# The mixer of a hybrid S5 and mLSTM layer: conv halo in the row, decay masked before the exp, S5 tables at half width copied by DMA, tokens of a block by position

## The chip, the cores and the metric

The kernel runs on one core of one Trainium2 chip. The core has five engines with queues of their own: PE (matrix products into PSUM), DVE (VectorE), ACT (ScalarE), POOL (GpSimd) and SP, which here issues all DMAs. Each engine takes its instructions in order, and semaphores make one engine wait for another. The metric is the time of one execution on the device in microseconds; lower is better. Times shown are medians of several runs; a profile is one more execution with the profiler on.

## What is computed

One layer (DEPTH = 1) over a sequence of 2048 tokens of width 1024, all in float32: a norm, one combined projection whose columns feed two mixers, an output projection, and a feed-forward block of width 4096.

```python
h = rmsnorm(x, norm_mix_g);  p = h @ w_in
u, q_raw, k_raw, v, o_raw, i_raw, f_raw = split(p)
# S5: 32 groups of 16 channels, 64 complex states a group
x_t = ab * x_{t-1} + (bb @ u_t)              # bb = s * b, complex, per group
y = Re(c @ x_t) + d * u
z = gelu(y); z = z * sigmoid(z @ w_glu + b_glu); y_ssm = rmsnorm(z)
# mLSTM: 4 heads of 128
q, k = split(silu(causal_conv_width_4([q_raw, k_raw]) + conv_b))
dmat = where(mask, bcum_t - bcum_s + i_s, -inf)
s = (q k^T) * exp(dmat - m_t)
num = s v + exp(inter - m_t) * (q C);  h = num / max(|den|, exp(-m_t))
C = decay * C + sum_s wk_s k_s v_s
y_ml = rmsnorm(sigmoid(o_raw) * h)
x = x + concat(y_ssm, y_ml) @ w_out
x = x + relu(rmsnorm(x) @ w_ff1)^2 @ w_ff2
out = rmsnorm(x)
```

## The kernel before

The sequence is cut into 4 blocks of 512 tokens (TB); with 4 heads that makes 16 mixer blocks, numbered b = 4 * head + token block. Products that must be near float32 are made of three float16 matmuls on a high and a low half of each operand (mm3, L152; its three lines are L156, L157, L158). Transposes and the small products of the mixers are float32 matmuls.

The program is written as Python that lists instructions; a planner then orders each engine's queue by its own model of time and sets the semaphores. So instructions of neighbouring steps lie mixed in each queue, and a buffer with `bufs=1` makes the next writer wait for the last reader.

In time order:

- **Start.** norm_x normalises and transposes x. u_proj makes S5's input u into uz, proj_vo and proj_qk start on the first blocks. s5_tables (L289) builds, on DVE, the powers of the state matrix (pwr, pwi) and cosine and sine tables: Lc, Ls, Hc, Hs hold the angles of 16 low and 16 high steps for all 32 groups on all 128 partitions; the lower 64 partitions stand for the real and the upper 64 for the imaginary part, and L403 turns the sign of Ls and Hs in the upper half.
- **Mixer blocks, 0 to 15** (the loop near the end of the mixer part). Block b has proj_qk for block b + 1 (L222), mix_store for block b - 1 (L879), mix_scores (L800), proj_vo (L245), mix_state (L827) and mix_out (L850). In blocks 0 to 10, 16 S5 units of two groups each are mixed in: s5_state(u) (L655), s5_const(u + 1) (L566) and s5_out(u) (L692), one or two units a block. In blocks 11 to 15 and after them come 16 GLU steps (glu_a, glu_b, glu_c), and the loads of the output weights (load_wo).
- **Output projection** (out_proj), with the last GLU steps beside it, and then the **feed-forward** block, over half of the time.

The steps that the change touches:

- *Conv in proj_qk.* The product pq lies in PSUM, channels by tokens. ACT makes y = w3 * pq + bias (L231). DVE adds the three other taps by shifted reads of pq (L233, 511, 510 and 509 columns), and after each the tap of the one to three columns that come from the block before (L235, from the tile hl, which L238 keeps). Then ACT's tanh (L241) and DVE's product (L242).
- *mix_scores.* bcm holds minus the running maximum, spread over partitions by DMA. For each of four chunks DVE makes min(bcm + g, 0) (L808), then ACT takes exp of all four at once (L812), and POOL sets what lies above the diagonal to 0 (L813, affine_select).
- *s5_const.* Per unit: one DMA of B and C for two groups (L580), seven small DVE instructions of 32 columns that scale them (six through the helper at L577, and L594), products with powers, two small PE steps, and the unit's cosT and sinT: 512 columns, three instructions on POOL (L574) and three on DVE (L577), each from L and H tables by broadcast. cosT and sinT have one buffer.
- *s5_state.* The product pw is turned by cosT and sinT (L676, L677, L678), scanned (L681), turned back (L685, L686). ACT exchanges the two halves of the partitions by copies (L674, L675, L683, L684); the sign is in the tables.
- *s5_out.* ACT squares py, DVE makes 0.044715 * y2 + 1 (L704) and multiplies by py (L705), ACT takes the tanh (L706), and so on.
- *glu_c.* The transposed GLU result is split into float16 halves in ms: L782 on ACT and L783 on DVE, both with the token index as outer and step 8 in the output.
- *mix_store.* The transposed head output is split likewise into mo (L887, L888), straight, and stored by DMA (L889).

## Time and profile before

| | |
|---|---|
| runs, median (3 runs) | 2251.63 us (2249.8 to 2255.08) |
| profiled execution, own time | 2252.2 us |
| its span, first to last instruction | 2250.5 us |
| mean granted clock of PE | 0.966 |
| matrix instructions, DVE, ACT, POOL instructions | 11021, 3087, 1799, 1039 |
| busy share of the span: PE, DVE, ACT, POOL | 92%, 81%, 47%, 50% |

How to read the views: a group's row gives line, engine, operation, out<-in with partitions x columns and type, its count, then busy microseconds in all and mean nanoseconds of one, then the idle time just ahead of it and who ended that. A row of the stretches gives start and end, the length, the busy time and number of instructions of each engine, the granted clock, the DMA engines' share and their GB/s. A row of the timeline gives start, duration, engine, line and the instruction. A busy PE is not a PE at its peak, since matmuls overlap in the record; how far apart they start tells what they cost. SPq is SP's sequencer, which issues DMAs.

### The profile page before, as it was taken

How to read it: one execution, taken by the hardware profiler on the slowest of the kernel's cores; microseconds unless marked ns; L12 is line 12 of the kernel's file. 1: busy time of each engine (PE TensorE's matmuls, PEld its weight loads, DVE VectorE, ACT ScalarE, POOL GpSimd, SP SyncE). 2: the span in 40 equal slices, each digit the busy share in tenths (PEclk: the TensorE clock that was granted, in tenths of full speed). 3: DMA queues.
4: the chain of work that ended last, by engine and by line, in shares of the span. 5: the costliest groups of instructions: out<-in, count | busy, mean ns of one | idle time of the engine just before them, and what ended most of it. 6: DMA issues, size and time to landing. Idle time of an engine off the chain costs nothing.

```text
span 2250.5 us, 29559 instructions
## 1 busy us (share of the span) xinstructions
PE 2063.3 (92%) x11021; PEld 1155.6 (51%) x11021; DVE 1813.9 (81%) x3087; ACT 1059.5 (47%) x1799; POOL 1132.4 (50%) x1039
## 2 busy tenths in 40 slices
...
GB/s 171 60 34 31 36 13 17 55 17 16 80 15 31 175 57 47 75 131 173 47 71 57 57 57 57 57 56 187 113 150 99 119 86 54 75 38 75 38 20 93
DMA packets 48624, 159.75 MB, mean 71 GB/s; under 512 B 6944, under 2 KB 16352, under 8 KB 35936
## 3 DMA queue, kind: packets, MB, share of 16 engines
...
## 4 chain that ended last, share of the span: by engine, by line
PE 50%; DVE 27%; DMA 6%; POOL 3%; issue 3%; ACT 3%; SPq 0%; POOLq 0%; DVEq 0%; ACTq 0%
PE gx L1281 4%; PE gx L1283 4%; PE gx L1282 4%; PE fx L1281 4%; PE fx L1282 4%; PE fx L1283 4%; PE gv L1281 2%; PE gv L1282 2%; PE gv L1283 2%; PE fv L1283 2%; PE fv L1282 2%; PE fv L1281 2%; DVE y L233 2%; DMA r<-in_w_dram 2%; PE po L156 2%
## 5 line engine op out<-in xcount | busy, mean ns | idle before, releaser
L1159 ACT ACTIVATE w2o<-r,fs_b 128x512 f16<-128x512 f32 (+1 forms) x128 | 105.4, 824 | 153.6 <-PE gx L1283 75.1
L1310 ACT ACTIVATE e<-e 128x512 f32<-128x512 f32 x96 | 60.3, 629 | 210.8 <-DVE e L1350 95.2
L1282 PEld LDWEIGHTS <-w2o 128*128 128x128 f16 x896 | 87.7, 98 | 132.2 <-issue 31.3
L1160 DVE SCALAR_TENSOR_TENSOR w2o<-r,fs_b,w2o 128x512 f16<-128x512 f32 (+1 forms) x128 | 130.3, 1019 | 27.3 <-ACT w2o L1159 27.1
L1281 PEld LDWEIGHTS <-w2o 128*128 128x128 f16 x896 | 87.9, 98 | 108.3 <-issue 2.9
L1283 PEld LDWEIGHTS <-w2o 128*128 128x128 f16 x896 | 87.7, 98 | 106.4 <-DVE w2o L1160 1.1
L156 PE MATMUL pv<-w_vo,xn 128*128 128x256 f16 x512 | 141.1, 276 | 0.3 <-ACT xn L433 0.3
L158 PE MATMUL pv<-w_vo,xn 128*128 128x256 f16 x512 | 140.9, 275 | 0.4 <-DVE xn L434 0.3
L157 PE MATMUL pv<-w_vo,xn 128*128 128x256 f16 x512 | 141.0, 275 | 0.0
L1216 POOL TENSOR_TENSOR r<-r,s 128x256 f32<-128x256 f32 x64 | 62.6, 978 | 130.5 <-DVE w2o L1160 129.2
L1380 DVE SCALAR_TENSOR_TENSOR x2b<-gx,dd,x2b 128x512 f32<-128x512 f32 x128 | 94.7, 744 | 41.2 <-PE gx L1283 41.0
L1281 PE MATMUL fx<-hop,wB 128*128 128x512 f16 x256 | 98.0, 383 | 9.8 <-ACT e L1339 7.7
L1380 DVE SCALAR_TENSOR_TENSOR x<-gx,dd,x 128x512 f32<-128x512 f32 x128 | 94.6, 743 | 14.7 <-PE gx L1283 14.6
L156 PE MATMUL pq<-xn,w_qk 128*128 128x512 f16 x256 | 99.1, 388 | 0.0
L158 PE MATMUL pq<-xn,w_qk 128*128 128x512 f16 x256 | 98.9, 386 | 0.0
L157 PE MATMUL pq<-xn,w_qk 128*128 128x512 f16 x256 | 98.6, 385 | 0.0
L1282 PE MATMUL fx<-hop,wB 128*128 128x512 f16 x256 | 98.0, 383 | 0.0
L1283 PE MATMUL fx<-hop,wB 128*128 128x512 f16 x256 | 97.8, 382 | 0.0
L157 PEld LDWEIGHTS <-xn 128*128 128x128 f16 x768 | 87.9, 115 | 11.2 <-issue 2.1
L1173 POOL TENSOR_TENSOR s<-r 128x512 f32<-128x512 f32 x32 | 55.3, 1729 | 76.0 <-issue 72.8
L156 PEld LDWEIGHTS <-xn 128*128 128x128 f16 x768 | 87.8, 114 | 10.7 <-ACT xn L433 1.2
L158 PEld LDWEIGHTS <-xn 128*128 128x128 f16 x768 | 87.7, 114 | 8.3 <-DVE xn L434 0.9
...
## 6 DMA issues: line engine op xcount, KB each, us to landing
...
hopd<-ho SPq DMA_DIRECT2D x28, 256.0 KB, 2.4
...
bcm<-negM_d SPq DMA_DIRECT2D x16, 256.0 KB, 3.2
ml_d<-mo SPq DMA_DIRECT2D x16, 256.0 KB, 2.3
```

Of the source, the lines that this page charges most:

```text
L156: T.matmul(out, wh, xh, start=(i == 0), stop=False)
L157: T.matmul(out, wh, xl, start=False, stop=False)
L158: T.matmul(out, wl, xh, start=False, stop=(i == n - 1))
L1159: S.activation(out=hi, in_=src, func=AF.Copy, scale=sg)
L1160: V.scalar_tensor_tensor(out=lo, in0=src, scalar=sg, in1=hi, op0=ALU.mult, op1=ALU.subtract)
L1173: G.tensor_tensor(out=s12[:, 0], in0=raw[:, 2], in1=raw[:, 3], op=ALU.add)
L1216: G.tensor_tensor(out=r[:, 1], in0=r[:, 1], in1=s12[:, 1], op=ALU.subtract)
L1281: T.matmul(out, wh, xh, start=(first and i == 0), stop=False, skip_group_check=True)
L1282: T.matmul(out, wh, xl, start=False, stop=False, skip_group_check=True)
L1283: T.matmul(out, wl, xh, start=False, stop=(last and i == n - 1), skip_group_check=True)
L1310: S.activation(out=x, in_=x if src is None else src, func=AF.Relu, scale=scale)
L1380: V.scalar_tensor_tensor(out=acc[:, j, c, :], in0=bk[b], scalar=dd, in1=acc[:, j, c, :], op0=ALU.mult, op1=ALU.add)
```

## The change

- *Conv.* ACT also copies pq into an SBUF row xc of 515 columns; the first three are the halo, copied by POOL from hl or set to zero at a head's first block, and POOL keeps the next halo from xc. The three taps then read xc over all 512 columns; the small taps and the copy on DVE go.
- *Decay.* POOL's affine_select comes first, from bcm with -1e30 above the diagonal; ACT then makes the exp per chunk with g as bias. The DVE step with its min goes.
- *S5 B/C.* Every fourth unit, s5_bc loads and scales B and C for eight groups at once.
- *Tables.* L and H tables are kept for one of a unit's two groups in each half of the partitions, so they are half as wide; a unit's cos and sin are made once as rh (256 columns each), and four DMAs copy them into rt, which has two buffers, once for each half of the partitions and group. The sign is no longer in the tables: two of ACT's copies take scale -1.
- *s5_out.* One DVE instruction makes (y2 + 1/0.044715) * py, and tanh's scale takes up the factor.
- *Token order.* Within a block of 512 tokens the order is by position within eight, then by eight: glu_c writes runs of 64, mix_store reads the transposed tile in steps of 8, and the host lays x and the output out to fit.

```diff
@@ -35,6 +35,7 @@
 S5_BLOCKS = 11
+RT_BUFS = 2
@@ -228,15 +229,20 @@
         wc = cw[:, 4 * w:4 * w + 4]
...
+        xc = mpa.tile([P, TB + 3], F32, name=f"xc{nm}{w}", tag="xc", bufs=2)
+        S.activation(out=xc[:, 3:], in_=pq, func=AF.Copy)
         S.activation(out=y, in_=pq, func=AF.Identity, scale=wc[:, 3:4], bias=cb[:, w:w + 1])
-        for j in range(1, 4):
-            V.scalar_tensor_tensor(out=y[:, j:], in0=pq[:, :TB - j], scalar=wc[:, 3 - j:4 - j], in1=y[:, j:], op0=ALU.mult, op1=ALU.add)
-            if t > 0:
-                V.scalar_tensor_tensor(out=y[:, 0:j], in0=halo[w][:, 3 - j:3], scalar=wc[:, 3 - j:4 - j], in1=y[:, 0:j], op0=ALU.mult, op1=ALU.add)
+        if t > 0:
+            G.tensor_copy(xc[:, 0:3], halo[w])
+        else:
+            G.memset(xc[:, 0:3], 0.0)
...
             hl = smal.tile([P, 3], F32, name=f"hl{nm}{w}", tag=f"hl{w}", bufs=2)
-            V.tensor_copy(hl, pq[:, TB - 3:TB])
+            G.tensor_copy(hl, xc[:, TB:TB + 3])
             halo[w] = hl
+        for j in range(1, 4):
+            V.scalar_tensor_tensor(out=y, in0=xc[:, 3 - j:3 - j + TB], scalar=wc[:, 3 - j:4 - j], in1=y, op0=ALU.mult, op1=ALU.add)
@@ -271,10 +277,10 @@
     pwi = cp.tile([P, 9, NG], F32, name="pwi")
-    Lc = cp.tile([P, 16, NG], F32, name="Lc")
-    Ls = cp.tile([P, 16, NG], F32, name="Ls")
-    Hc = cp.tile([P, 16, NG], F32, name="Hc")
-    Hs = cp.tile([P, 16, NG], F32, name="Hs")
+    Lc = cp.tile([P, 16, 16], F32, name="Lc")
+    Ls = cp.tile([P, 16, 16], F32, name="Ls")
+    Hc = cp.tile([P, 16, 16], F32, name="Hc")
+    Hs = cp.tile([P, 16, 16], F32, name="Hs")
@@ -384,23 +390,26 @@
-            t3 = dp.tile([P, 8, NG], F32, name="t3")
...
+            cs2, sn2 = (dp.tile([P, 8, 16], F32, name=f"d_{n}") for n in ("cs2", "sn2"))
+            for o_, i_ in ((cs2, cs), (sn2, sn)):
+                for g in range(2):
+                    hp_ = slice(64 * g, 64 * g + 64)
+                    V.tensor_copy(o_[hp_], i_[hp_, 1:9].rearrange("p l (u g) -> p l g u", g=2)[:, :, g])
+            t3 = dp.tile([P, 8, 16], F32, name="t3")
...
                     n = 1 << l
-                    ec = cs[:, 1 + 4 * b + l, :].unsqueeze(1).to_broadcast([P, n, NG])
-                    es = sn[:, 1 + 4 * b + l, :].unsqueeze(1).to_broadcast([P, n, NG])
+                    ec = cs2[:, 4 * b + l, :].unsqueeze(1).to_broadcast([P, n, 16])
+                    es = sn2[:, 4 * b + l, :].unsqueeze(1).to_broadcast([P, n, 16])
...
                     add(s_[:, n:2 * n], s_[:, n:2 * n], t3[:, :n])
-            for s_ in (Ls, Hs):
-                fl = s_.rearrange("p l g -> p (l g)")
-                V.tensor_scalar(out=fl, in0=fl, scalar1=sgn, scalar2=None, op0=ALU.mult)
@@ -562,6 +571,24 @@
     s5 = s5_ctx.enter_context(pool("s5"))
+    bcs = {}
...
+    def s5_bc(v):
...
+        bcA = bcs[v] = s5.tile([P, 4, 8, 16], F32, name=f"bcA{v}", tag="bcA", bufs=2)
+        nc.sync.dma_start(out=bcA, in_=s5bc[:, :, 8 * v:8 * v + 8, :])
+        bt = [s5.tile([P, 8, 16], F32, name=f"bt{v}{i}", tag="bt", bufs=2) for i in range(2)]
...
+        def mul(o, a, b):
+            V.tensor_tensor(out=o, in0=a, in1=b[:, 8 * v:8 * v + 8].unsqueeze(2).to_broadcast([P, 8, 16]), op=ALU.mult)
...
+        mul(bt[0], bcA[:, 1], ssi)
+        mul(bt[1], bcA[:, 0], sim)
+        mul(bcA[:, 0], bcA[:, 0], sre)
+        mul(bcA[:, 1], bcA[:, 1], ssr)
+        V.tensor_tensor(out=bcA[:, 0], in0=bcA[:, 0], in1=bt[0], op=ALU.add)
+        V.tensor_tensor(out=bcA[:, 1], in0=bcA[:, 1], in1=bt[1], op=ALU.subtract)
+        V.tensor_scalar(out=bcA[:, 2], in0=bcA[:, 2], scalar1=sgn, scalar2=None, op0=ALU.mult)
@@ -576,22 +603,9 @@
-        bc = st("bc", (4, 2, 16), 2)
-        nc.sync.dma_start(out=bc, in_=s5bc[u])
...
-        eb, fb, tb_ = st("eb", (2, 16)), st("fb", (2, 16)), st("tb", (2, 16))
...
-        def b16(a):
-            return a[:, gs].unsqueeze(2).to_broadcast([P, 2, 16])
...
-        vtt(eb, bc[:, 0], b16(sre), ALU.mult)
-        vtt(tb_, bc[:, 1], b16(ssi), ALU.mult)
-        vtt(eb, eb, tb_, ALU.add)
-        vtt(fb, bc[:, 1], b16(ssr), ALU.mult)
-        vtt(tb_, bc[:, 0], b16(sim), ALU.mult)
-        vtt(fb, fb, tb_, ALU.subtract)
-        cg = st("cg", (2, 16))
-        V.tensor_scalar(out=cg, in0=bc[:, 2], scalar1=sgn, scalar2=None, op0=ALU.mult)
+        if u % 4 == 0:
+            s5_bc(u // 4)
+        eb, fb, cg, cx = (bcs[u // 4][:, i, 2 * (u % 4):2 * (u % 4) + 2, :] for i in range(4))
@@ -633,22 +647,26 @@
-        cosT, sinT = st("cosT", (2, 16, 16), 1), st("sinT", (2, 16, 16), 1)
-        tc_, td_ = st("t1", (2, 16, 16)), st("t2", (2, 16, 16))
+        rh = st("rh", (2, 16, 16))
+        tc_, td_ = (st(t, (2, 16, 16))[:, 0] for t in ("t1", "t2"))
...
         def hk(a):
-            return a[:, :, gs].rearrange("p k g -> p g k").unsqueeze(3).to_broadcast([P, 2, 16, 16])
+            return a[:, :, u].unsqueeze(2).to_broadcast([P, 16, 16])
...
         def ll(a):
-            return a[:, :, gs].rearrange("p k g -> p g k").unsqueeze(2).to_broadcast([P, 2, 16, 16])
...
-        gtt(cosT, hk(Hc), ll(Lc), ALU.mult)
+            return a[:, :, u].unsqueeze(1).to_broadcast([P, 16, 16])
...
+        gtt(rh[:, 0], hk(Hc), ll(Lc), ALU.mult)
         gtt(tc_, hk(Hs), ll(Ls), ALU.mult)
-        gtt(cosT, cosT, tc_, ALU.subtract)
-        vtt(sinT, hk(Hs), ll(Lc), ALU.mult)
+        gtt(rh[:, 0], rh[:, 0], tc_, ALU.subtract)
+        vtt(rh[:, 1], hk(Hs), ll(Lc), ALU.mult)
         vtt(td_, hk(Hc), ll(Ls), ALU.mult)
-        vtt(sinT, sinT, td_, ALU.add)
-        s5u[u] = xt, m0, inT, cosT.rearrange("p g k l -> p (g k l)"), sinT.rearrange("p g k l -> p (g k l)")
+        vtt(rh[:, 1], rh[:, 1], td_, ALU.add)
+        rt = st("rt", (2, 2, 256), RT_BUFS)
+        for g in range(2):
+            for h in range(2):
+                nc.sync.dma_start(out=rt[64 * h:64 * h + 64, g], in_=rh[64 * g:64 * g + 64].rearrange("p s k l -> p s (k l)"))
+        s5u[u] = xt, m0, inT, rt[:, :, 0, :], rt[:, :, 1, :]
@@ -669,24 +687,23 @@
             T.matmul(pw_[:, g, :], inT[:, g, :], us[:, g].rearrange("p h c -> p (h c)"), start=True, stop=True)
-        wf = pw_.rearrange("p g c -> p (g c)")
-        t1, t2 = st("t1", (512,)), st("t2", (512,))
-        S.copy(t2[0:64], wf[64:128])
-        S.copy(t2[64:128], wf[0:64])
-        V.tensor_tensor(out=t1, in0=wf, in1=cosF, op=ALU.mult)
...
+        t1, t2 = st("t1", (2, 256)), st("t2", (2, 256))
+        S.copy(t2[0:64], pw_[64:128])
+        S.activation(out=t2[64:128], in_=pw_[0:64], func=AF.Copy, scale=-1.0)
+        V.tensor_tensor(out=t1, in0=pw_, in1=cosF, op=ALU.mult)
...
         for g in range(2):
-            gc = slice(g * 256, (g + 1) * 256)
-            V.tensor_tensor_scan(out=t1[:, gc], data0=R8[:, g0 + g:g0 + g + 1].to_broadcast([P, 256]), data1=t1[:, gc], initial=0.0, op0=ALU.mult, op1=ALU.add)
-        t2 = st("t2", (512,))
+            V.tensor_tensor_scan(out=t1[:, g], data0=R8[:, g0 + g:g0 + g + 1].to_broadcast([P, 256]), data1=t1[:, g], initial=0.0, op0=ALU.mult, op1=ALU.add)
+        t2 = st("t2", (2, 256))
         S.copy(t2[0:64], t1[64:128])
-        S.copy(t2[64:128], t1[0:64])
+        S.activation(out=t2[64:128], in_=t1[0:64], func=AF.Copy, scale=-1.0)
...
         G.memset(sv[:, :, 0:1], 0.0)
-        G.tensor_tensor(out=sv[:, :, 1:257], in0=t1.rearrange("p (g c) -> p g c", g=2), in1=t2.rearrange("p (g c) -> p g c", g=2), op=ALU.subtract)
+        G.tensor_tensor(out=sv[:, :, 1:257], in0=t1, in1=t2, op=ALU.subtract)
@@ -701,9 +718,8 @@
         S.activation(out=y2, in_=py, func=AF.Square)
-        V.tensor_scalar(out=y2, in0=y2, scalar1=0.044715, scalar2=1.0, op0=ALU.mult, op1=ALU.add)
-        V.tensor_tensor(out=y2, in0=y2, in1=py, op=ALU.mult)
-        S.activation(out=y2, in_=y2, func=AF.Tanh, scale=GC)
+        V.scalar_tensor_tensor(out=y2, in0=y2, scalar=1.0 / 0.044715, in1=py, op0=ALU.add, op1=ALU.mult)
+        S.activation(out=y2, in_=y2, func=AF.Tanh, scale=GC * 0.044715)
@@ -778,9 +794,10 @@
             T.transpose(pT[:, m, :], zc[:, m * P:(m + 1) * P], ident)
-        mv = ms[h].rearrange("p s m (c i) -> p s i m c", i=8)
-        S.activation(out=mv[:, 0, i], in_=pT, func=AF.Copy)
-        V.tensor_tensor(out=mv[:, 1, i], in0=pT, in1=mv[:, 0, i], op=ALU.subtract)
+        mv = ms[h].rearrange("p s m (b i c) -> p s i m b c", b=2, i=8)
+        pv_ = pT.rearrange("p m (b c) -> p m b c", b=2)
+        S.activation(out=mv[:, 0, i], in_=pv_, func=AF.Copy)
+        V.tensor_tensor(out=mv[:, 1, i], in0=pv_, in1=mv[:, 0, i], op=ALU.subtract)
@@ -804,13 +821,14 @@
         sc = mpb.tile([P, 4, P], F32, name=f"sc{b}", tag="sc")
...
+        G.affine_select(out=dm, in_=bcm, pattern=[[0, 4], [1, P]], compare_op=ALU.is_ge, fill=-1e30, base=0, channel_multiplier=-1)
         for c in range(4):
-            V.tensor_scalar(out=dm[:, c, :], in0=bcm[:, c, :], scalar1=gcol[:, 0, r0 + c:r0 + c + 1], scalar2=0.0, op0=ALU.add, op1=ALU.min)
...
             mix_load(b + 1)
-        S.activation(out=dm, in_=dm, func=AF.Exp)
-        G.affine_select(out=dm, in_=dm, pattern=[[0, 4], [1, P]], compare_op=ALU.is_ge, fill=0.0, base=0, channel_multiplier=-1)
+        for c in range(4):
+            S.activation(out=dm[:, c, :], in_=dm[:, c, :], func=AF.Exp, bias=gcol[:, 0, r0 + c:r0 + c + 1])
@@ -882,10 +900,11 @@
             T.transpose(pT[:, c, :], og[:, c, :], ident)
-        pTf = pT.rearrange("p c t -> p (c t)")
+        pTf = pT.rearrange("p c (r i) -> p i (c r)", i=8)
         mo = mpb.tile([P, 2, TB], F16, name=f"mo{b}", tag="mo", bufs=2)
-        S.activation(out=mo[:, 0, :], in_=pTf, func=AF.Copy, scale=XS)
-        V.scalar_tensor_tensor(out=mo[:, 1, :], in0=pTf, scalar=XS, in1=mo[:, 0, :], op0=ALU.mult, op1=ALU.subtract)
+        mv = mo.rearrange("p s (i c) -> p s i c", i=8)
+        S.activation(out=mv[:, 0], in_=pTf, func=AF.Copy, scale=XS)
+        V.scalar_tensor_tensor(out=mv[:, 1], in0=pTf, scalar=XS, in1=mv[:, 0], op0=ALU.mult, op1=ALU.subtract)
@@ -1482,7 +1501,8 @@
     a["xN"] = c(f["x"][0])
-    a["xT"] = c(f["x"][0].T)
...
+    a["xT"] = c(f["x"][0].T.reshape(D, NTB, 64, 8).transpose(0, 1, 3, 2).reshape(D, SEQ))
@@ -1521,7 +1541,7 @@
     st = np.stack([np.concatenate(t, 0) for t in ((br, bi), (bi, br), (cr, ci), (ci, cr))], 1)
-    a["s5bc"] = c(st.reshape(P, 4, 16, 2, 16).transpose(2, 0, 1, 3, 4))
+    a["s5bc"] = c(st.reshape(P, 4, NG, 16))
@@ -1547,4 +1567,5 @@
     got = r.results[0]["out_0_dram"]
+    got = got.reshape(D, NTB, 8, 64).transpose(0, 1, 3, 2).reshape(D, SEQ)
```

2 lines of the change are left out of this document (1 added, 1 removed).

## Prediction, made before the changed kernel was run

> **What bounds the kernel now.** I read the page's chain first, then the busy time of the engines by stretches of the span, then the groups of DVE's and PE's instructions inside the stretch that stood out.
>
> ```profile
> PE 50%; DVE 27%; DMA 6%; POOL 3%; issue 3%; ACT 3%; SPq 0%; POOLq 0%; DVEq 0%; ACTq 0%
> ```
>
> PE holds half of the chain and DVE a quarter. An average says little here, so the span is cut where the program changes its work: the mixer with the S5 units (168 to 590 us, blocks 0 to 10), the mixer with the GLU (590 to 784), the output projection (784 to 896), the rest.
>
> ```profile
> core 0: us, PE busy (x) PEld busy (x) DVE busy (x) ACT busy (x) POOL busy (x), PEclk, DMA share, GB/s
> 56.00:168.00 112.00, 107.94 (x896) 99.81 (x895) 91.32 (x344) 37.58 (x72) 21.08 (x29) 0.97 0.14 47
> 168.00:590.00 422.00, 376.71 (x2524) 285.94 (x2523) 402.71 (x855) 201.01 (x474) 244.38 (x245) 0.96 0.09 30
> 590.00:712.00 122.00, 113.11 (x743) 78.52 (x742) 94.47 (x213) 50.96 (x105) 23.50 (x27) 0.97 0.11 40
> 712.00:784.00 72.00, 41.94 (x243) 29.00 (x242) 51.87 (x120) 29.67 (x59) 19.24 (x19) 0.72 0.38 139
> 784.00:896.00 112.00, 112.00 (x549) 54.53 (x548) 63.16 (x84) 40.22 (x50) 7.85 (x11) 1.00 0.15 50
> ```
>
> From 168 to 590 us DVE is busy 402.7 of 422 us (95%): this stretch is DVE's. PE is at 89% there and waits on DVE's results. From 784 us PE never stops, so what the change does to the six GLU steps that lie there is hidden by PE, and nothing after 896 us is touched. The question is how far DVE falls in the long stretch and what PE then needs by itself.
>
> PE's own need comes from counts (of the groups by line; pv and pq have three lines each, L156 to L158, with these counts within 1) and from the distance of starts where PE runs without a gap.
>
> ```profile
> L158 PE MATMUL pv<-w_vo,xn 128*128 128x256 f16 x348 | 95.9, 276 | 0.0
> L158 PE MATMUL pq<-xn,w_qk 128*128 128x512 f16 x174 | 67.9, 390 | 0.0
> ```
>
> ```profile
> 334.99 0.38 PE L632 MATMUL pit<-ident,inm 128*128 128x128 f32 x2
> 335.21 0.38 PE L156 MATMUL pq<-xn,w_qk 128*128 128x512 f16 x1
> 335.43 0.38 PE L157 MATMUL pq<-xn,w_qk 128*128 128x512 f16 x1
> ...
> 340.85 0.40 PE L699 MATMUL py<-m,us 128*128 128x128 f32 x2
> 341.08 0.59 PE L700 MATMUL py<-xt,sv 128*128 128x128 f32 x2
> 341.50 0.40 PE L699 MATMUL py<-m,us 128*128 128x128 f32 x2
> ```
>
> A pq matmul starts 0.22 us after the last (335.21, 335.43), so a pv matmul, with half the columns, 0.11; the four py matmuls from 340.85 to 341.50 take 0.65 us, and the transposes and small fp32 ones 0.11 us each (pit's two from 334.99 to 335.21). So pq 520 x 0.22 = 114, pv 1046 x 0.11 = 115, py 16 units of 16, 256 x 0.163 = 42, and the other 702 of the 2524 x 0.11 = 77, with 7 more for the 64 of pw, which are twice as wide: **355 us**. So PE could do this stretch in 355 us; it takes 422. At most 67 us are to be had here.
>
> **The change part by part, in the long stretch.** These are DVE's groups there that the change touches.
>
> ```profile
> L233 DVE SCALAR_TENSOR_TENSOR y<-pq,cw,y 128x511 f32<-128x511 f32 (+2 forms) x66 | 48.6, 736 | 0.0
> ...
> L577 DVE TENSOR_TENSOR sinT<-Hs,Lc 128x512 f32<-128x512 f32 x15 | 22.1, 1476 | 0.0
> L629 DVE SCALAR_TENSOR_TENSOR m<-Jm,ct,m 128x128 f32<-128x128 f32 x30 | 21.5, 754 | 1.1 <-ACT m L627 1.1
> L577 DVE TENSOR_TENSOR t<-Hc,Ls 128x512 f32<-128x512 f32 x15 | 21.1, 1405 | 0.1
> L242 DVE SCALAR_TENSOR_TENSOR y<-th,y 128x512 f32<-128x512 f32 x22 | 19.4, 882 | 0.2
> L235 DVE SCALAR_TENSOR_TENSOR y<-hl,cw,y 128x1 f32<-128x1 f32 (+2 forms) x51 | 19.3, 378 | 0.0
> L808 DVE TENSOR_SCALAR dm<-bcm,gcol 128x128 f32<-128x128 f32 x44 | 15.4, 403 | 0.0
> L577 DVE TENSOR_TENSOR sinT<-sinT,t 128x512 f32<-128x512 f32 x15 | 14.1, 939 | 0.1
> ...
> L577 DVE TENSOR_TENSOR fb<-fb,tb 128x32 f32<-128x32 f32 x14 | 7.6, 545 | 0.1
> L704 DVE TENSOR_SCALAR y<-y 128x512 f32<-128x512 f32 x16 | 7.5, 472 | 0.1
> ...
> L577 DVE TENSOR_TENSOR fb<-bc,ssr 128x32 f32<-128x32 f32 x13 | 3.3, 250 | 0.0
> ```
>
> *Conv.* The halo taps L235 go: -19.3 (the halo copy moves to POOL as well; I leave its small time out). The 66 taps L233 change their first operand from PSUM to the SBUF row xc. The same operation with two SBUF operands and 512 columns is L242, at 0.882 where the taps have 0.736: 66 x 0.146 = +9.6, which I take; if they ran free of POOL they could be no dearer than now, so 0 is the other end. The first tap now also waits for POOL's copy of three columns into xc and for ACT's copy of pq. Behind that tap, in DVE's queue, stand the updates of C for which PE waits. ACT pays 22 more copies of 512 columns, 10 to 16 us at 0.47 to 0.74 (L704, L233), out of the 221 us that it idles here.
>
> The Trainium skill's page "GPSIMD Engine Reference", section "1. Specifications", says that GpSimd shares its SBUF interfaces with VectorE and that the two get in each other's way when a DVE instruction has two SBUF inputs or runs in a two-port mode; by it the taps, which have one SBUF input now, join that class, which speaks against this edit. The trace agrees (0.882 of L242 against 0.736 of L233); the sum by the rule is the +9.6 above, without it 0.
>
> *Decay.* The 44 TENSOR_SCALAR of L808 go: -15.4. POOL's select comes first with the same size, and one ACT exp over 512 columns becomes four over 128, on ACT: 44 x 0.4, 18 us at the most, of the same idle time. The exps now wait for POOL; behind them on ACT stand the copies of pv and pq, whose PSUM tiles PE needs back, and each can be late by one POOL instruction. How such a TENSOR_SCALAR suffers is seen once:
>
> ```profile
> 316.09 5.32 DVE L808 TENSOR_SCALAR dm<-bcm,gcol 128x128 f32<-128x128 f32 x4
> ```
>
> and on POOL, the last of the instructions that it ran in that time:
>
> ```profile
> 320.01 1.32 POOL L814 TENSOR_TENSOR sc<-sc,y 128x512 f32<-128x512 f32 x1
> ```
>
> Four of them took 5.32 us, against 1.6 at the mean of 0.403, and ended within 0.1 us of POOL's instruction (321.41 and 321.33). I read it as DVE's busy time holding time in which it waits for POOL; then fewer such instructions, and less work on POOL, both shorten it.
>
> *S5 B/C for eight groups.* Per unit six small TENSOR_TENSOR (the dearest and the cheapest stand above, 7.6 and 3.3; the six together 30) go: -30; the sign flip L594 goes too and is left out as small. Seven of 128 columns per four units come, three times in this stretch: 21 x 0.403 (L808's row, the same size) = +8.4; the bounds are 0.25 (the cheapest small one) and 0.754 (L629, two SBUF operands of 128 columns), so +5 to +16. One DMA takes the place of four.
>
> *Tables.* The three DVE instructions per unit (22.1 + 21.1 + 14.1 = 57.3) get half the columns. A fixed part stays, so I put 31 in place of 57.3: **-26**. If their time were all waits for POOL they would stay as they are, 0; at half it is -29. POOL's three table instructions halve likewise. Four DMAs of 128 KB per unit come on SP's queue, from SBUF to SBUF, between the last table instruction and the product that reads it.
>
> *y2.* L704 goes (-7.5); the new instruction has the form of L705, which it replaces.
>
> *Token order.* mix_store reads PSUM at a stride of 8 and writes straight. No row shows a strided PSUM read; a strided SBUF read, L746 below, costs about 0.4 us more than the 0.472 of L704 at the same size. 10 x 0.4 = +4, on ACT as much; bounds 0 and 10 x 1.7 (what the strided f16 write L783, below, costs over L233).
>
> The sign that moves from the tables into two of ACT's copies costs no instruction: 0. The sum: -19.3 + 9.6 - 15.4 - 30 + 8.4 - 26 - 7.5 + 4 = **-76 us** of 403; -29 with the dear end of every part, -96 with the cheap ones. DVE then needs 327 us, less than PE's 355. So PE becomes the bound, and the gain is not 76. How closely PE is then kept busy is read from 56 to 168 us: there DVE is busy 82% (327 of 392 is 83%), and PE 96%. 376.7 / 0.96 = 392: **-30 us** here.
>
> *The GLU stretch.*
>
> ```profile
> by line: ACT ms L782 13.3%; DMA st_out<-in_wout_dram 10.5%; DVE st_out L131 9.7%; DVE ms L783 6.8%; DVE mx_out L104 6.2%; issue 6.1%; DVE gth L763 2.9%; ACT gth L764 2.6%; PE pgl L158 2.4%; DVE zc L771 2.4%; DVE zt L752 2.4%; PE pgT L780 2.
> ```
>
> and of the groups from 590 to 800 us, DVE's and then ACT's:
>
> ```profile
> L783 DVE TENSOR_TENSOR ms<-pgT,ms 128x512 f16<-128x512 f32 x10 | 24.5, 2450 | 8.5 <-ACT ms L782 8.4
> ...
> L746 DVE TENSOR_SCALAR zc<-uz,zs 128x512 f32<-128x512 f32 x13 | 12.4, 968 | 0.0
> ```
>
> ```profile
> L782 ACT ACTIVATE ms<-pgT 128x512 f16<-128x512 f32 x10 | 24.6, 2462 | 15.3 <-PE pgT L780 15.3
> ```
>
> The first line is the chain of waits from 712 to 784 us. L782 and L783 write f16 in steps of 8 elements; after the change they write runs of 64. The nearest row of that many columns from PSUM is L233, 0.736: seven tenths of each go. On that chain they hold 20% of 72 us, 14.5, so **-10**. What is late next is the load of w_out (its DMA, L131 and L104 hold 26% of the chain), which the change doesn't touch; if it ends the waits anyway, 0. From 590 to 712 us PE is at 93%, and at most the 9 us that it idles could go; I count none of them, and 7 for the range. Ahead of 168 us the tables of s5_tables are built half as wide, PE idles 4 us of 112 there: **-1** of these.
>
> In all -41 from the profiled execution's 2252.2 us (its span is 2250.5, 1.7 lie around it; the median of the runs shown, 2251.63, is the same within 0.03%): **2211 us**.
>
> **The rivals.**
> 1. *PE runs almost without gaps.* Its waits in the long stretch are for results of a late DVE; with 76 us less of work ahead of them the clock (0.96) also rises. 355 / 0.97 = 366 is -56; with the whole -17 and -3 (s5_tables): 2176. For it: tables have two buffers now and can be made a unit ahead. Against: 590 to 712 us, where DVE has 77% and PE only 93%.
> 2. *DVE waits where it worked.* The first tap of each conv stands in DVE's queue until POOL has copied three columns, and POOL takes its queue in order, an instruction of 1.3 us at a time and busy 58%. Behind that tap lie the state updates that PE waits for. 22 x 1 us or so, with the taps at 0.882 and PE at 92%: 376.7 / 0.92 = 409, -13 here, little in the GLU stretch: 2238.
> 3. *The edits take no weight off what sets the end:* 2251, if the strided writes are slow for another reason and PE's waits stay.
> 4. *Slower: the transfers of the tables come late.*
>
> ```profile
> L580 SPq DMA_DIRECT2D bc<-in_s5bc_dram x13: 327/328/333, 167.6 to 475.6; - x13
> ```
>
> and of the page's DMA issues:
>
> ```profile
> ml_d<-mo SPq DMA_DIRECT2D x16, 256.0 KB, 2.3
> ```
>
> An issue takes 0.33 us of SP, and 256 KB land 2.3 us later. Four issues and such a landing are 3.6 us per unit; if each of the 15 units of the stretch showed it on DVE, whose queue stops at the product with cosF, and PE behind it, that is 54 us against the 41 gained: 2265. On SP the four also stand ahead of mo's store, bcm's load and the weight loads until the tables are ready. It decides from 41 / 15 = 2.7 us per unit on. Against it: SP is idle most of the time, the tables are due one unit later, and there are two buffers.
>
> **How the numbers follow.** The forecast (2195 to 2225) 0.55; rival 1 0.18; rival 2 0.14; rival 3 0.04; rival 4 0.09. Faster by over 0.2% (about what a measurement of this kernel can tell from no change) is the first three: 0.87; within it 0.04; slower 0.09. The range goes from rival 1 to just past rival 2, 2176 to 2240, and leaves out rivals 3 and 4 and a little of 1.
>
> **What would show it.** In the changed kernel's profile: DVE's busy share of the mixer-and-S5 stretch near 80% and PE's over 95%; the stretch about 390 us long; no L235 or L808; ms writes near 0.6 us on both engines; taps between 0.74 and 0.9 us. Wrong if DVE shows idle time ahead of the taps that POOL ends (rival 2) or ahead of the product with cosF that a DMA ends (rival 4), if the strided read of pT costs over 1 us, or if the stretch is DVE's still.

## The result and the profile after

| | before | after |
|---|---|---|
| median of the runs (us) | 2251.57 (2249.8 to 2255.08, 4 runs) | 2200.80 (2200.19 to 2201.49, 4 runs) |
| ratio after / before, 95% interval | | 0.9773 [0.9756, 0.979] |
| profiled execution, its span (us) | 2252.2, 2250.5 | 2201.49, 2199.5 |

The change takes 51 us off. In the two traces the time between landmarks of the program tells where. A landmark is the first instruction that writes the named tile; the last column is the forecast.

| from, to | before | after | difference | forecast |
|---|---|---|---|---|
| start, first put | 168.6 | 165.6 | -3.0 | -1 |
| first put, m_glu (S5 stretch) | 424.6 | 399.1 | -25.5 | -30 |
| m_glu, first po (GLU) | 186.0 | 169.7 | -16.3 | -10 |
| first po, first fx (output projection) | 202.1 | 201.1 | -1.0 | 0 |
| first fx, end (feed-forward) | 1269.1 | 1264.0 | -5.1 | 0 |

The chain of waits of the changed kernel, by engine, on its page:

```profile
PE 56%; DVE 22%; DMA 7%; POOL 5%; ACT 3%; issue 3%; SPq 1%; POOLq 0%; DVEq 0%; ACTq 0%
```

PE has 56% where it had 50, DVE 22 where it had 27, and POOL has come up from 3 to 5. The busy times by stretches of the changed kernel, with the cuts at the same landmarks:

```profile
core 0: us, PE busy (x) PEld busy (x) DVE busy (x) ACT busy (x) POOL busy (x), PEclk, DMA share, GB/s
56.00:165.00 109.00, 105.51 (x899) 99.02 (x900) 87.14 (x338) 40.01 (x79) 22.50 (x36) 1.00 0.18 56
165.00:564.00 399.00, 368.22 (x2509) 283.61 (x2508) 329.90 (x645) 216.11 (x528) 230.31 (x282) 0.97 0.18 52
564.00:672.00 108.00, 105.31 (x731) 74.45 (x730) 76.97 (x168) 48.77 (x120) 25.84 (x37) 1.00 0.11 40
672.00:734.00 62.00, 39.28 (x251) 28.49 (x250) 44.90 (x115) 22.82 (x60) 18.06 (x18) 0.80 0.44 161
```

DVE has 329.9 of 399 us in the S5 stretch, 83%. PE has 92%, not the 97% that it keeps ahead of it. The column in which the two stretches differ most is POOL's: 22.5 of 109 us there, 230 of 399 here. PE's work differs too: 762 of its 899 matrix instructions ahead of the stretch are those of one projection, pu, and it idles 3.5 us there, while in the stretch it has the small products of the S5 units and the mixer as well, and idles 30.8. The S5 stretch of the kernel before, between the same landmarks:

```profile
168.00:593.00 425.00, 379.71 (x2543) 287.82 (x2542) 405.67 (x860) 202.01 (x476) 245.39 (x246) 0.96 0.09 31
```

Set against it, PE idles 14.5 us less (45.3 and 30.8), and its own busy time is 11.5 us shorter: 34 matrix instructions fewer fall into the stretch, and the granted clock is 0.97 instead of 0.96. So not all of the gain is waits that went. The groups of DVE in the S5 stretch of the changed kernel that answer to the rows of before:

```profile
L245 DVE SCALAR_TENSOR_TENSOR y<-xc,cw,y 128x512 f32<-128x512 f32 x65 | 59.8, 921 | 1.7 <-ACT y L235 1.5
...
L643 DVE SCALAR_TENSOR_TENSOR m<-Jm,ct,m 128x128 f32<-128x128 f32 x30 | 15.6, 558 | 7.1 <-ACT m L641 7.1
...
L604 DVE TENSOR_TENSOR t<-Hc,Ls 128x256 f32<-128x256 f32 x15 | 11.5, 767 | 5.3 <-POOL sv L706 5.3
...
L604 DVE TENSOR_TENSOR rh<-Hs,Lc 128x256 f32<-128x256 f32 x14 | 11.4, 816 | 14.1 <-DMA rt<-rh 14.1
...
L604 DVE TENSOR_TENSOR rh<-rh,t 128x256 f32<-128x256 f32 x15 | 9.4, 624 | 0.2
...
L907 DVE SCALAR_TENSOR_TENSOR mo<-pT,mo 128x512 f16<-128x512 f32 x10 | 6.8, 676 | 0.0
```

The halo taps and the decay's TENSOR_SCALAR are gone, the tables cost 32.3 us, the taps 0.921 us each, and there is a new wait of 14.1 us for the rt transfers. The strided read of PSUM in mix_store costs nothing (0.676 us). The writes of ms, from 564 to 760 us, on DVE and on ACT:

```profile
L800 DVE TENSOR_TENSOR ms<-pgT,ms 128x512 f16<-128x512 f32 x11 | 7.5, 683 | 0.6 <-ACT ms L799 0.6
...
L799 ACT ACTIVATE ms<-pgT 128x512 f16<-128x512 f32 x11 | 6.5, 591 | 17.8 <-PE pgT L796 17.8
```

They took 2.45 and 2.46 us before. In the stretch where they stood on the chain, 672 to 734 us now, the chain is led by the load of w_out, as forecast:

```profile
by line: DMA st_out<-in_wout_dram 19.2%; POOL w_out L135 7.7%; DVE mx_out L105 7.4%; DVE st_out L132 7.1%; PE pn L879 3.9%; PE pn L881 3.6%; PE pgl L159 3.5%; PE pgl L157 3.0%; issue 2.9%; PE pgl L158 2.8%; DVE zc L787 2.8%; PE pst L858 2.4
```

### The profile page after: what moved, and what is told of

Same layout as the page of the kernel before. It is cut to its first block, busy times and chain, and to the rows that moved or that the text cites. A ratio compares the mean times of both kernels' runs of the same rounds, so it can differ in the third digit from the quotient of the medians.

```text
span 2199.5 us, 29564 instructions
## 1 busy us (share of the span) xinstructions
PE 2045.9 (93%) x11021; PEld 1148.6 (52%) x11021; DVE 1702.6 (77%) x2829; ACT 1055.5 (48%) x1879; POOL 1125.3 (51%) x1095
## 3 DMA queue, kind: packets, MB, share of 16 engines
q1 hardware_dynamic: 53408, 166.26, 22.5%
## 4 chain that ended last, share of the span: by engine, by line
PE 56%; DVE 22%; DMA 7%; POOL 5%; ACT 3%; issue 3%; SPq 1%; POOLq 0%; DVEq 0%; ACTq 0%
PE gx L1300 4%; PE gx L1302 4%; PE gx L1301 4%; PE fx L1300 4%; PE fx L1301 4%; PE fx L1302 4%; PE gv L1300 2%; PE gv L1302 2%; PE gv L1301 2%; PE fv L1302 2%; PE fv L1300 2%; PE fv L1301 2%; PE po L157 2%; PE po L158 2%; PE po L159 2%
## 5 line engine op out<-in xcount | busy, mean ns | idle before, releaser
L1399 DVE SCALAR_TENSOR_TENSOR x<-gx,dd,x 128x512 f32<-128x512 f32 x128 | 94.7, 743 | 14.7 <-PE gx L1302 14.5
```

The costliest lines, as they stand in the source:

```text
L1399: V.scalar_tensor_tensor(out=acc[:, j, c, :], in0=bk[b], scalar=dd, in1=acc[:, j, c, :], op0=ALU.mult, op1=ALU.add)
```

## The experiments

Each run was timed against the kernel before on its own chip. "Cost" below is (its ratio - 0.9773) x 2252 us, its distance from the changed kernel. With both intervals (about 0.0017 and 0.0015, added as squares) a cost is good to about 5 us, so that costs under 5 are not told from zero. Every edit also makes the planner (the scheduler of the expectations) order the queues anew, and the length of a stretch can move by 5 us for that alone (u_order below).

### Undoing one part at a time

*Tables.* The tables of both groups on all partitions, 512 columns an instruction, without rt transfers:

```
-        gtt(rh[:, 0], hk(Hc), ll(Lc), ALU.mult)
...
-                nc.sync.dma_start(out=rt[64 * h:64 * h + 64, g], ...)
+        gtt(cosT, hk(Hc), ll(Lc), ALU.mult)
...
+        vtt(sinT, sinT, td_, ALU.add)
```

> The changed kernel with its table part undone alone: tables for both groups on all partitions, 512 columns an instruction, sign in the tables, no rt transfers. DVE gets back 57 - 32 = 25 us of the three table instructions per unit, and loses the 16 us in which it waits for rt transfers (14.1 + 1.7). Theory (DVE was the bound of the S5 stretch, PE is now, so the parts overlap and none is worth its own DVE time): DVE near 355 us in the stretch, the stretch 5 to 10 us longer than 399, total 2206 to 2211. Rival 1 (this part carries the gain): 18 us or more longer, 2219 and up. Rival 2 (the transfers give back what the half tables save): no longer or shorter, 2193 to 2202.

Measured: 2227.63 us, ratio 0.9888 [0.9873, 0.9902], cost +25.9. Rival 1 holds: this part alone is worth half of the gain, and the S5 stretch is back at 424.1 us, where it was before the change, with all other parts in place. The S5 stretch of u_tables:

```profile
167.00:591.00 424.00, 377.74 (x2509) 292.39 (x2507) 377.73 (x646) 216.18 (x528) 265.80 (x283) 0.94 0.09 30
```

DVE rose by 48 us and POOL by 35, though the table instructions give back only 32 and 27. The rest is in rows that the edit doesn't touch, and PE's waits say what it did to PE. First DVE's m row of u_tables, then POOL's table rows, then PE's waits in u_tables, longest first:

```profile
L641 DVE SCALAR_TENSOR_TENSOR m<-Jm,ct,m 128x128 f32<-128x128 f32 x30 | 23.4, 819 | 6.6 <-ACT m L639 6.6
```

```profile
L599 POOL TENSOR_TENSOR t<-Hs,Ls 128x512 f32<-128x512 f32 x15 | 27.1, 1809 | 0.2
...
L599 POOL TENSOR_TENSOR cosT<-Hc,Lc 128x512 f32<-128x512 f32 x15 | 22.8, 1517 | 4.6 <-DVE t L696 1.9 <-DVE v L884 1.7 <-DVE rc L878 1.1
L599 POOL TENSOR_TENSOR cosT<-cosT,t 128x512 f32<-128x512 f32 x15 | 21.2, 1413 | 0.3
```

```profile
engine line waited for: us in total, times, longest us
PE pT L896 <- POOL sv L699: 11.6, 2, 6.5
PE pT L896 <- POOL og L889: 10.3, 4, 4.7
PE py L711 <- POOL sv L700: 7.3, 4, 3.2
PE pgg L632 <- DVE t L688: 4.5, 2, 4.3
PE py L711 <- POOL xc L239: 3.1, 2, 2.2
```

The same view of the changed kernel:

```profile
PE py L717 <- POOL sv L706: 4.5, 4, 1.9
PE pn L879 <- DVE C L863: 4.2, 3, 2.0
PE pT L902 <- POOL og L895: 4.0, 3, 2.3
PE pgg L634 <- DVE t L694: 3.4, 1, 3.4
PE pgg L634 <- DVE uz L724: 3.0, 1, 3.0
PE pit L646 <- DVE uz L724: 2.6, 2, 1.8
PE pT L902 <- POOL sv L705: 2.5, 2, 2.4
```

m went from 0.558 to 0.819 us with nothing of its own changed, and PE's longest waits are now for POOL: for og and sv, in whose queue the wide table products stand. All of PE's waits in the stretch, added up by the engine that ended them, show what moved:

| us of PE's waits, ended by | DVE | ACT | POOL |
|---|---|---|---|
| before | 25.5 | 11.1 | 8.7 |
| changed kernel | 16.7 | 1.7 | 12.4 |
| u_tables | 10.4 | 3.5 | 32.3 |

So 15.5 of the 25 us are waits. The other 9.5 are PE's own busy time (377.7 against 368.2 for the same 2509 matrix instructions), at a granted clock of 0.94 against 0.97; why the clock differs is not shown. One rival is left untested: the part also gives cos and sin a second buffer, which u_tables takes away, and no run has wide tables with two. The waits that one buffer causes directly in u_tables are small: 1.9 us of POOL's cosT for DVE's t (L696, in the row above), and 1.2 of DVE's sinT for POOL's t.

*B/C.* Six small TENSOR_TENSOR, a sign flip and a transfer per unit again, with the old host layout:

```
-        if u % 4 == 0:
-            s5_bc(u // 4)
+        bc = st("bc", (4, 2, 16), 2)
+        nc.sync.dma_start(out=bc, in_=s5bc[u])
...
+        vtt(eb, bc[:, 0], b16(sre), ALU.mult)
```

> The changed kernel with only the B/C part undone: six small TENSOR_TENSOR and one TENSOR_SCALAR per unit and one small transfer per unit, in place of seven of 128 columns per four units. DVE gets back 30 + 3 - 6 to 17, some 20 us, in the stretch. Theory (PE is the bound now, parts overlap): 3 to 8 us longer, 2204 to 2209. Rival 1 (this part carries the gain, since the small chain stands at the head of each unit): 15 us or more, 2216 and up. Rival 2 (nothing hangs on it): within 2 us of 2201.

Measured: 2204.45 us, ratio 0.9785 [0.9771, 0.98], cost +2.7. DVE is 22.6 us up in the stretch (352.46 of 401 us), as expected, and the stretch is 1.3 us longer: the theory's lower end by time, and not told from zero. The small instructions cost DVE time and almost no time of the kernel.

*Conv.* Taps from PSUM and halo taps on DVE again:

```
-        S.activation(out=xc[:, 3:], in_=pq, func=AF.Copy)
...
-            V.scalar_tensor_tensor(out=y, in0=xc[:, 3 - j:3 - j + TB], ...)
+            V.scalar_tensor_tensor(out=y[:, j:], in0=pq[:, :TB - j], ...)
+            if t > 0:
+                V.scalar_tensor_tensor(out=y[:, 0:j], in0=halo[w][:, 3 - j:3], ...)
```

> The changed kernel with only the conv part undone: taps from PSUM of 509 to 511 columns, halo taps of 1 to 3 columns on DVE, halo copy on DVE, no xc. DVE gets back 19 us of halo taps and 2 to 4 of the halo copy, and loses 65 x (0.921 - 0.736) = 12 us on the taps; ACT loses 13 us of copies, POOL its halo copies. Theory (PE is the bound, parts overlap; the dear taps give most of this part back): within 5 us of the changed kernel, 2199 to 2206. Rival 1 (this part carries the gain): 15 us or more, 2216 and up. Rival 2 (two SBUF operands beside POOL cost more than the halo taps saved): shorter by 3 us or more, 2198 and below.

Measured: 2196.82 us, ratio 0.9747 [0.9731, 0.9763], cost -5.9: rival 2, at the edge of what can be told. The conv part gives nothing, and may take a little. Its stretch, and one line's instructions (count, then ns least / median / most) for the taps of u_conv and of the changed kernel:

```profile
164.00:559.00 395.00, 367.46 (x2510) 284.77 (x2508) 329.89 (x712) 206.69 (x507) 210.38 (x244) 0.97 0.18 52
```

```profile
L234 DVE SCALAR_TENSOR_TENSOR y<-pq,cw,y x72: 714/737/751, 168.8 to 588.4; 128x511 f32<-128x511 f32 x24, 128x510 f32<-128x510 f32 x24, 128x509 f32<-128x509 f32 x24
```

```profile
L245 DVE SCALAR_TENSOR_TENSOR y<-xc,cw,y x65: 717/745/1815, 170.6 to 562.6; 128x512 f32<-128x512 f32 x65
```

DVE's total is the same to 0.1 us with 51 halo taps and the halo copies more, and POOL's is 20 us less. From PSUM a tap takes 0.714 to 0.751 us whatever runs beside it. From SBUF half of them take as little, and others up to 1.815. Laid over POOL's instructions in the trace from 160 to 600 us, the SBUF taps with no POOL work beside them take 0.74 us in the mean (21 of 72, none over 0.752), and those with some 0.97 (51); the PSUM taps take 0.74 in both cases (30 alone, 42 beside POOL).

*Decay.* Four TENSOR_SCALAR on DVE, one exp, the select last:

```
-        G.affine_select(out=dm, in_=bcm, ..., fill=-1e30, ...)
+            V.tensor_scalar(out=dm[:, c, :], in0=bcm[:, c, :], scalar1=gcol[...], scalar2=0.0, op0=ALU.add, op1=ALU.min)
...
+        S.activation(out=dm, in_=dm, func=AF.Exp)
+        G.affine_select(out=dm, in_=dm, ..., fill=0.0, ...)
```

> The changed kernel with only the decay part undone: four TENSOR_SCALAR of DVE per block, one exp of 512 columns, POOL's select last. DVE gets back 44 x 0.4 = 15 us or a little more in the stretch and as much per block up to the 15th. Theory (PE is the bound, parts overlap): 2 to 7 us longer, 2203 to 2208. Rival 1 (this part carries the gain, since the four stand ahead of the product with pS and the values of pn): 15 us or more, 2216 and up. Rival 2 (the select ahead of the exps makes ACT late and gives it back): within 1 us or shorter, 2197 to 2202.

Measured: 2216.32 us, ratio 0.9838 [0.9823, 0.9853], cost +14.6: rival 1, at its lower end. The stretch is 9.2 us longer and the GLU part 3.6. The line of the four, in u_decay, on DVE:

```profile
L825 DVE TENSOR_SCALAR dm<-bcm,gcol x48: 271/280/1373, 180.1 to 593.2; 128x128 f32<-128x128 f32 x48
```

Half of them take 0.28 us or less and the dearest 1.37; with POOL at work beside them (28 of the 48) they take 0.82 us in the mean, alone (20) 0.28. The 44 in the stretch come to 24.9 us, not the 15.4 of the forecast.

*Token order.* ms and mo, xT and the output in the order of the sequence:

```
-        mv = ms[h].rearrange("p s m (b i c) -> p s i m b c", b=2, i=8)
...
+        mv = ms[h].rearrange("p s m (c i) -> p s i m c", i=8)
...
```

> The changed kernel with the token order undone alone: ms written in steps of 8 elements again, mo and xT in the order of the sequence. ACT's and DVE's ms writes back at 2.45 us from 0.59 and 0.68. Theory (the strided writes set the GLU stretch, 16.3 us shorter after the change): the time from m_glu to the first po 14 to 18 us longer, the rest equal, total 2215 to 2219. Rival 1 (a part of those 16 us comes from the lighter S5 stretch and the weight loads, as forecast with 10): 2209 to 2213. Rival 2 (the load of w_out sets the end of it anyway): within 3 us of 2201.

Measured: 2215.58 us, ratio 0.9839 [0.9824, 0.9854], cost +14.9: the theory by time. From m_glu to the first po it takes 182.6 us, 12.9 more, a little under the theory's 14; the S5 stretch is 394.6, 4.5 less, with nothing there but mo's form changed. ms on ACT and on DVE in u_order:

```profile
L798 ACT ACTIVATE ms<-pgT 128x512 f16<-128x512 f32 x9 | 22.1, 2458 | 11.9 <-PE pgT L796 11.9
```

```profile
L799 DVE TENSOR_TENSOR ms<-pgT,ms 128x512 f16<-128x512 f32 x9 | 22.1, 2453 | 11.5 <-ACT ms L798 11.5
```

### One part alone

The kernel before with the table part only:

> The kernel before with the table part alone (tables of one group per half of the partitions, rt transfers, two buffers); conv, decay, B/C, y2 and token order as before. If the parts add up, the time is that of the changed kernel plus what each other part cost when undone: 2200.8 + 14.9 (order) + 14.6 (decay) + 2.7 (B/C) - 5.9 (conv) + some 2 (y2) = 2229, a gain of 22 us. Theory (POOL's three table products stand in POOL's queue ahead of sv and og, for which PE waits, and DVE's beside them; the part is worth the same alone): 2226 to 2234, DVE still above 85% of its S5 stretch, PE's waits for sv and og no longer than in the kernel before. Rival (DVE was the one bound: 25 us off its 403 alone gives at most a third of what the sum of the parts gave, 8 us, and PE takes over only with the rest): 2241 to 2246.

Measured: 2234.09 us, ratio 0.9915 [0.9896, 0.9934], 19 us faster than before. The parts add up within the intervals: the five costs are 25.9 + 2.7 - 5.9 + 14.6 + 14.9 = 52.2 us, against a gain of 51.1 (y2 was not undone by itself). Its S5 stretch, 407.3 us long, and two rows of DVE there:

```profile
163.00:571.00 408.00, 372.32 (x2529) 287.25 (x2527) 358.73 (x856) 201.82 (x474) 204.69 (x246) 0.97 0.18 52
```

```profile
L632 DVE SCALAR_TENSOR_TENSOR m<-Jm,ct,m 128x128 f32<-128x128 f32 x30 | 16.5, 590 | 4.3 <-ACT m L630 4.3
L243 DVE SCALAR_TENSOR_TENSOR y<-th,y 128x512 f32<-128x512 f32 x22 | 16.3, 742 | 0.4 <-ACT th L242 0.4
```

Over the same landmarks DVE had 405.7 us before and POOL 245.4: 47 and 41 less. The table instructions of DVE are 29 of those 47 (57.3 to 28.3); m fell from 0.754 to 0.590 and the last step of the conv from 0.882 to 0.742, untouched by the edit. One expectation missed: PE waits 11.5 us for og here, 3.8 before.

### Load on one engine

Three more products of 256 columns per unit, into a tile that nobody reads, on DVE and, in another kernel, on POOL:

```
+        sx = st("sx", (16, 16))
+        for a_, b_ in ((Hs, Lc), (Hc, Ls), (Hc, Lc)):
+            vtt(sx, hk(a_), ll(b_), ALU.mult)
```

> The changed kernel with three more products of 256 columns per unit on DVE, into a tile that nobody reads, of the forms and operands of the table instructions: 15 x 3 x 0.7 = some 32 us more of DVE in the S5 stretch, which is what undoing the table part gave back to DVE's three table rows (64.1 against 32.3). Theory A (the table part's 27 us come from DVE and POOL getting in each other's way: load on either engine costs about the same): the stretch 8 to 15 us longer, total 2209 to 2217. Theory B (DVE alone): 20 us or more, 2220 and up, and the same load on POOL next to nothing. Theory C (POOL alone): within 4 us of 2201.

> The changed kernel with three more products of 256 columns per unit on POOL, into a tile that nobody reads: 15 x 3 x 1.0 = some 45 us more of POOL, against the 27 us (71.1 against 44.0) that undoing the table part gave back to POOL. Theory A (load on either engine costs about the same): 12 to 22 us longer, 2213 to 2223, with the rows of DVE's SBUF products dearer than in the changed kernel. Theory B (DVE alone): within 4 us of 2201. Theory C (POOL alone, by its own place in the unit's chain): 20 us or more, with DVE's rows as dear as in the changed kernel.

Measured: load_dve 2218.31 us, ratio 0.9851 [0.9835, 0.9868], cost +17.6; load_pool 2215.78, ratio 0.9841 [0.9826, 0.9855], cost +15.3. The second is within theory A by time, the first 1 us above it; but the load didn't stand where it was meant to. One tile's instructions, in load_dve and then in load_pool:

```profile
L604 DVE TENSOR_TENSOR sx<-Hs,Lc x16: 577/594/1012, 143.2 to 201.8; 128x256 f32<-128x256 f32 x16
```

```profile
L601 POOL TENSOR_TENSOR sx<-Hs,Lc x16: 765/882/1218, 133.2 to 225.8; 128x256 f32<-128x256 f32 x16
```

Nothing waits for sx, and the planner issued all 48 products by 207 us on DVE (32.0 us) and by 234 on POOL (42.8 us). So the runs show that in the first blocks a us of DVE costs 0.55 us (17.6 / 32.0), and one of POOL 0.36 (15.3 / 42.8): neither engine is slack. These are not prices of one engine alone: in load_pool DVE is busy 340.9 us in the S5 stretch, 11 more, with none of its instructions changed. They don't show the price over the whole stretch, nor how the gain of the tables divides between DVE and POOL.

### The wait for the transfers

The new wait of rh for rt (14.1 us on DVE, 18.9 on POOL) looked like a loss. First a second buffer, then the products kept out of rh:

```
-        rh = st("rh", (2, 16, 16))
+        rh = st("rh", (2, 16, 16), 2)
```

> The changed kernel with two buffers in place of one for rh, so that the next unit's table products need not wait until the transfers have read the last. The waits for rt transfers ahead of rh (14.1 us on DVE, 18.9 on POOL, 0.0 of the rest changed) go. Theory (these waits stand in both queues ahead of work that PE needs): 3 to 8 us shorter, 2193 to 2198. Rival (the two engines sit idle there anyway, and only wait elsewhere): within 2 us of 2201.

```
...
-        vtt(rh[:, 1], hk(Hs), ll(Lc), ALU.mult)
-        vtt(td_, hk(Hc), ll(Ls), ALU.mult)
-        vtt(rh[:, 1], rh[:, 1], td_, ALU.add)
+        vtt(t2_[:, 1], hk(Hs), ll(Lc), ALU.mult)
+        vtt(t2_[:, 0], hk(Hc), ll(Ls), ALU.mult)
+        vtt(rh[:, 1], t2_[:, 1], t2_[:, 0], ALU.add)
```

> The changed kernel with the four products of the tables written into halves of t1 and t2 that are free at that point, so that rh is written by the last two instructions alone. In the run with two buffers the scheduler put the first product of a unit one unit further ahead, directly behind the transfers that free its buffer, and the waits stayed (11.3 us on DVE, 17.8 on POOL). Theory (those waits are of the queue's order, and hold up both engines): the waits of rh for rt transfers fall below 5 us on each engine and the time by 3 to 8 us, 2193 to 2198. Rival 1 (the idle time is slack and reappears ahead of another instruction): within 2 us of 2201. Rival 2 (the products now wait for t1 and t2, which the state of the unit before still holds): 2203 or more.

Measured: rh_two 2196.72 us, ratio 0.976 [0.9745, 0.9774], cost -2.9; rh_late 2201.29, ratio 0.9769 [0.9746, 0.9792], cost -0.9. DVE's waits in rh_two and in rh_late:

```profile
DVE rh L604 <- DMA rt<-rh: 11.3, 5, 5.0
DVE C L863 <- PE pst L858: 10.6, 4, 4.2
```

```profile
DVE C L863 <- PE pst L858: 9.1, 4, 4.7
DVE t L604 <- POOL sv L706: 7.0, 3, 2.5
DVE m L643 <- ACT m L641: 6.6, 8, 1.1
```

With two buffers the planner put the first product one unit further ahead, behind the transfers that free the other buffer, and the wait stayed; its time is within the theory's range, but the wait that was to explain that is there, and the 2.9 us aren't told from zero. In rh_late DVE's wait ahead of rh is gone, and the time is the same: rival 1 of rh_late holds. POOL's idle time in the stretch is what it was (172 us, 169 in the changed kernel), and now stands ahead of other instructions. DVE's fell from 69 to 59 us, but its busy time rose by 6 (335.88 us), and the stretch, 3.7 us shorter, is within what a new order alone moves. So the wait was where idle time showed, and a kernel without it gained nothing that can be told (this run's cost is good to about 6 us).

### Less load on POOL and DVE

> The changed kernel with the product of og and v4 (11 in the stretch, 1.29 us each on POOL, 14.2 us) as four copies with a scale on ACT, which idles 183 of 399 us there. Theory (POOL's queue is a bound beside DVE: 45 us of load added to it cost 15): 14 us less on POOL give 3 to 7 us, and PE's wait for og falls from 4.0 us to 1 or less, 2194 to 2198. Rival (PE waits for og because of what comes before it, v4's pow on POOL, and the copies queue on ACT): within 2 us of 2201 or slower.

```
-        G.tensor_tensor(out=og, in0=og, in1=v4.unsqueeze(2).to_broadcast([P, 4, P]), op=ALU.mult)
+        for c in range(4):
+            S.activation(out=og[:, c, :], in_=og[:, c, :], func=AF.Copy, scale=v4[:, c:c + 1])
```

Measured: 2197.92 us, ratio 0.9761 [0.9742, 0.978], cost -2.7: the theory's upper end by time, and not told from zero. PE's wait for og, expected at 1 us or less, is 7.5 us, for ACT now:

```profile
PE pT L903 <- ACT og L896: 7.5, 10, 1.8
```

The S5 stretch is 2.4 us shorter. From m_glu to the first po, where blocks 11 to 15 have the same product, the trace has 160.2 us, 9.5 less than the changed kernel's; the feed-forward takes 5.0 more in it.

The last run joins this with a conv that has neither the halo taps nor the SBUF taps:

```
+        if t > 0:
+            V.tensor_tensor(out=y[:, 0:3], in0=y[:, 0:3], in1=halo[w], op=ALU.add)
+        for j in range(1, 4):
+            V.scalar_tensor_tensor(out=y[:, j:], in0=pq[:, :TB - j], scalar=wc[:, 3 - j:4 - j], in1=y[:, j:], op0=ALU.mult, op1=ALU.add)
+        if t < NTB - 1:
...
+            S.activation(out=hv, in_=pq[:, h0:TB], func=AF.Copy, scale=wc[:, 0:1])
+            for c, k, i in ((0, 1, 1), (1, 2, 1), (0, 2, 2)):
+                S.activation(out=hv[:, c:c + 1], in_=pq[:, h0 + k:h0 + k + 1], func=AF.Identity, scale=wc[:, i:i + 1], bias=hv[:, c:c + 1])
```

> The changed kernel with two edits on grounds of the runs. The taps read PSUM again (0.736 in the kernel before), without xc and without POOL's halo copies; the three halo taps become one sum of three columns that ACT makes a block ahead in four small instructions from pq's last three columns, and DVE adds in one instruction: 17 small DVE instructions in the stretch in place of 51 and the copies. And og's product on ACT as in the run og_on_act. Undoing the conv part gave 4 to 6 us, og on ACT 3, and 34 halo taps less at 0.378 are 13 us of DVE, at a third 4 us. Theory (DVE's and POOL's loads both count, about a third of a us for one us): DVE near 318 us and POOL near 195 in the stretch, 10 to 14 us shorter, 2187 to 2191. Rival 1 (PE's own need and its waits for ACT, which now carries og and the halo sums, end it): 2193 to 2198. Rival 2 (the instructions of three columns on ACT make y and the exps late): 2200 or more.

Measured: 2186.74 us (2184.83 to 2192.04, 5 runs), ratio 0.9712 [0.9696, 0.9727], cost -13.7. This is just below the theory's 2187 to 2191. It beats both kernels: 2.9% under the kernel before, and 0.9712 / 0.9773 = 0.994 of the changed one. Its S5 stretch is 384.3 us long:

```profile
164.00:548.00 384.00, 358.57 (x2466) 277.02 (x2465) 315.71 (x659) 229.73 (x603) 189.72 (x232) 0.98 0.19 53
```

DVE is at 315.7 us and POOL at 189.7, near the 318 and 195 expected, and PE has 93%. Of PE's waits there POOL ends only 2.6 us, DVE 10.5 and ACT 12.2. The run joins two edits, and says nothing of either alone.

## Why the prediction was right, and where it was not

The forecast was 2211 us, 41 us off, in a range of 2176 to 2240; the kernel took 51 off. The sign, the direction (work leaves DVE, PE comes nearer to its own need) and the two places (S5 stretch and GLU) were right. How the S5 stretch was to give its 30 us was not, and that the figure came out near is in part luck. Point by point:

- **DVE's 327 us.** It has 329.9. The terms of the sum: tables 32.3 us where 31 was forecast; B/C 22.6 by u_bc8, where 30 - 8.4 = 21.6 was; the taps 0.921 instead of 0.882, 12 us dearer and not 9.6; the strided read of PSUM 0 instead of +4 (the rows that its 0.4 us was read from, L746 and L704, differ by 0.5); the decay 24.9 us (u_decay) instead of 15.4. Between the same landmarks DVE fell by 75.8 us where 76 were forecast. Most terms were near; that the sum is that near is luck too, since rows that no part touches moved with it (m from 0.754 to 0.558 us).
- **The gain of 30 from PE's 96%.** The stretch became 399.1, a gain of 25.5. The forecast kept PE's 376.7 us of work and raised PE's share to 96%. The share reached 92%; with the work unchanged that is 376.7 / 0.92 = 409, a gain of 13, the figure of rival 2. The rest came from a term that the forecast put at nothing: PE's busy time itself fell by 11.5 us. Two errors offset each other here, and two of the signs that the forecast named, PE over 95% and a stretch of about 390 us, are missing. The step that failed is the analogy: "there DVE is busy 82% [...], and PE 96%". That stretch has DVE's load but not POOL's (19% against 58% in the kernel before), and it doesn't have PE's work either: 759 of 896 matrix instructions are of pu, and PE idles 4 of 112 us there. Which of the two makes the 92% isn't shown. POOL was named in the forecast only as something that makes DVE's instructions dear, and PE waits for POOL itself, for sv and og above all: 12.4 of its 30.8 us in the changed kernel, where DVE ends 16.7. But in taps_psum_hv POOL ends only 2.6, and PE is still at 93%. The price of a part didn't go by how much DVE time it held: 48 us of DVE and 35 of POOL cost the stretch 25 in u_tables, 20 of DVE cost 9 in u_decay, 23 of DVE cost 1 in u_bc8.
- **One sum for all parts.** The forecast added up DVE's time and then let PE end it, so that no part had a worth of its own. The runs gave each one, and these add up to the gain: tables 26, order 15, decay 15, B/C 3, conv -6. That the tables carry half was in no sum, because their effect on POOL was "halve likewise", without a number.
- **Conv.** Costed as -19.3 + 9.6 on DVE, with the halo copy's small time left out. DVE's saving and loss came out even (329.9 both with and without), and the part put 20 us on POOL. The rule of the Trainium skill that was weighed here ("GPSIMD Engine Reference", section "1. Specifications", on the interfaces that GpSimd and VectorE share) is borne out: the taps with two SBUF operands take 0.74 us alone and 0.97 in the mean beside POOL, and those from PSUM 0.74 in both cases.
- **GLU, -10.** It was -16.3. The term is mis-sized: u_order puts 12.9 on the strided writes, and u_decay 3.6 on the decay, whose blocks 11 to 15 lie here and which had no term in this stretch (3.6 is within what a new order alone moves). The load of w_out is next, as named.
- **Start, -1.** It was -3.
- **Nothing after 896 us.** The feed-forward took 5.1 us less in the profiled execution. Its code is the same in all these kernels, and their profiles show 1262.7 (load_dve and rh_two) to 1272.3 us (tables_alone) for it, u_order's with the old token order 1265.1. So this is no doing of the change that the runs could tie to a part; what sets it stays open.
- **Rival 1** (nearly gapless, 2176) was too far: the best of the runs has PE at 93%. Its 355 us for PE's need isn't contradicted: PE is busy 358.6 us there, with 58 matrix instructions fewer in the stretch than were counted for it.
- **Rival 2** (taps that wait for POOL's copies, PE at 92%) had PE's share right and the mechanism wrong: DVE idles 1.7 us ahead of the taps. What POOL does to the taps is to make them longer.
- **Rival 4** (late transfers, slower) is partly in the trace: an issue on SP takes 0.59 us and not 0.33, and both engines idle ahead of rh until a transfer lands. But rh_late takes that wait of DVE's away, and gains nothing that can be told. It would have been wrong to subtract it from the gain.

What is not settled: why the same DVE time costs nearly nothing at the head of a unit (B/C) and half its length in the decay (the parts stand in different places, but no run moved one part's place alone); how the tables' gain divides between DVE, POOL and the second buffer; and what sets PE's granted clock in the stretch.
